# Attention layers: the output product recorded in eight planned pieces between the rounds, and the last two groups of the second layer tile by tile

## The chip, the cores and the metric

The kernel runs on one core of one Trainium2 chip. The metric is device microseconds of one execution; less is better. It is given as the median of several runs.

## The reference, cut to what matters

Three transformer layers run one after the other on 256 tokens (two tiles of 128) of width 1024, all in 32-bit floats. The change touches the ends of the first two, each of which is attention over 16 heads of width 64, an output product, and a residual sum:

```python
# layer A (top-k picked keys), dsa_mixer
out = lax.map(block, ...)              # softmax(q k + bias, masked) v, by block of 128 queries
out = from_blocks(out).reshape(b, s, A_HEADS * A_HEAD_DIM)
return out @ w_o                       # 1024 x 1024
# layer B (low-rank keys and queries), mla_mixer
out = from_blocks(out).reshape(b, s, B_HEADS * V_DIM)
return out @ w_o                       # 1024 x 1024
# first_block, for both
h = h + mixer(rms_norm(h, g), ...)
h = h + sq_relu_mlp(rms_norm(h, mlp_norm[layer]), mlp_w_up[layer], mlp_w_down[layer])
```

A third layer (gated recurrence and windowed attention) and its feed-forward follow; the change leaves them as they are.

## The kernel before, in words

The code records instructions; a scheduler then orders each engine's list, with code that is recorded earlier as the more urgent, and sets the waits. Every engine works its own list from front to back.

**Products.** Every weight block of 512 rows by 512 columns (1 MB) is loaded by SyncE into a `raw` buffer and split in two halves: `whi` = a rounded copy, two ACT instructions of 1024 columns (L252), and `wlo` = `raw` minus `whi`, two DVE instructions (L255). There are 3 `raw` and 4 `whi`/`wlo` buffers. The other operand is split the same way after its transposes (L169: the high part on ACT, the low part on DVE). A product is three matmuls for each 128 rows: hi·hi (L275), hi·lo (L276), lo·hi (L278), 512 columns each, into one of two `acc` banks.

**Attention.** `att_step` (layer A) and `attend` (layer B) cut attention into steps of three functions: f1 makes logits (`lg`), the row maximum (`mx`, `nb`, `nx` on DVE) and the exponentials (`p` or `lg` on ACT, L493); f2 transposes them (`tr`, L165) and copies the result to `pT`, in turn on ACT (L500) and DVE (L502); f3 multiplies by the values into the one `po` bank (L509). `stages` runs f1 of a step beside f2 of the step before and f3 of the one before that; one such turn is a round. A finished half of 512 features is divided by the row sums (`o` L697, `oB` L888), transposed and split into `oT` (`aoh`/`aol` in layer A, `boh`/`bol` in layer B). There are two `tr` banks and three `lg` banks.

**Order.** `weave` walks a plan, a string: a star is a round, `*4` four of them, `**` the rest; the other words are items: projections, `k3` and `q3` (layer B's products for head group 3), `33` (transposes of its keys and queries into `KTb` and `QT`, L846 and L850), `o10` (transposes of tile 1, half 0). `out_proj` follows as one call, after the whole plan: it loads the four weight blocks of `w_o`, then computes for each tile both halves of the outputs over all eight feature blocks, and adds each to the residual `h` (L318). The MLP that follows takes the first weight blocks of `mlp_w_up` in the buffers that `w_o` leaves, and norms, transposes and splits `h` (`hn` L191, `mxh`/`mxl` L169).

Of the kernel before, what the change touches and what calls it, by code (L numbers as in the profile page):

```python
# [24 lines left out]
NACC, NTR, NLG, NPO = 2, 2, 3, 1  # L25


PLAN_A = "s0 k0 q0 q1 t00 t01 s1 * t10 k1 *4 t11 **"
PLAN_B = "k0 q0 k2 20 q1 k1 30 21 *2 q2 31 * 22 k3 q3 *2 32 *4 23 *2 o00 33 *5 o10 *2 o01 o11"
PLAN_C = "ck mg ms cq q0 mw k0 mn v0 v1 ml B0 *2 q1 *3 B1 *3 o0 k1 *3 k2 * v2 * q2 B2 o1 *2 a0 *2 a1 * b1 * p0 p1 *4 b0 *3"  # L30


# [57 lines left out]
def block_kernel(ctx: ExitStack, tc: tile.TileContext, a, out: bass.AP):  # L90
    nc = tc.nc
    V, A, G, PE = nc.vector, nc.scalar, nc.gpsimd, nc.tensor
# [9 lines left out]
    def nm(s):  # L102
        uid[0] += 1
        return f"{s}_{uid[0]}"
# [20 lines left out]
    def acc(s):  # L125
        return pp.tile([P, 512], F32, tag="acc", name=nm(s), bufs=NACC)
# [34 lines left out]
    def transposes(src, n, ps=None, w=P):  # L161

        ps = trp("tr") if ps is None else ps
        for i in range(n):
            PE.transpose(ps[:w, i * P:(i + 1) * P], src[:, i * w:(i + 1) * w], ident)  # L165
        return ps
# [32 lines left out]
    @contextmanager  # L199
    def behind(ins):  # L200

        with ExitStack() as st:
            for i in ins or ():
                st.enter_context(tc.issue_after(i.ins))
            yield

    def norm_x(x, gain, fold=True):


        holds, rs = [tuple(mark[1:])], []  # L210
        for t in range(2):
            if fold:
                rs.append(rms_stats(hres[t]))
                norm_T(hres[t], None, gain, x, t)
            else:
                norm_T(hres[t], rms_stats(hres[t]), gain, x, t)
            holds.append(tuple(mark))
        return holds, rs

    def xpair(s, kt=8):  # L220

        if kt == 2:
            b = t4(s, F32R).rearrange("p (e k n) -> p e k n", e=2, k=2)
            return [b[:, 0]], [b[:, 1]]

        def part(sfx):
            return [t4(s + sfx, F32R, n * 256).rearrange("p (k n) -> p k n", k=n)
                    for n in (min(4, kt - g) for g in range(0, kt, 4))]
        return part("h"), part("l")
# [5 lines left out]
    def xs(x, k, t):  # L235
        return x[k // 4][:, k % 4, t * P:(t + 1) * P]

    def wsplit(w, k0, kk, c0, n, gain=None, by_k=False):
        raw = wp.tile([P, 2048], F32, tag="raw", name=nm("raw"), bufs=NRAW)
        hi = wp.tile([P, 2048], F32R, tag="hi", name=nm("whi"), bufs=NHL)  # L240
        lo = wp.tile([P, 2048], F32R, tag="lo", name=nm("wlo"), bufs=NHL)
        m = kk * n
        if by_k:
            for k in range(kk):
                nc.sync.dma_start(raw[:, k * n:(k + 1) * n], w[(k0 + k) * P:(k0 + k + 1) * P, c0:c0 + n])
        else:
            nc.sync.dma_start(raw[:, :m].rearrange("p (k n) -> p k n", k=kk),
                              w[k0 * P:(k0 + kk) * P, c0:c0 + n].rearrange("(k p) n -> p k n", p=P))
        if gain is None:
            for i in range(2):  # L250
                c = slice(i * m // 2, (i + 1) * m // 2)
                A.activation(hi[:, c], raw[:, c], AF.Copy)  # L252
            for i in range(2):
                c = slice(i * m // 2, (i + 1) * m // 2)
                V.tensor_tensor(lo[:, c], raw[:, c], hi[:, c].bitcast(F32), op=OP.subtract)  # L255
        else:
            for k in range(kk):
                c = slice(k * n, (k + 1) * n)
                gk = gain[:, k0 + k:k0 + k + 1]
                A.activation(hi[:, c], raw[:, c], AF.Copy, scale=gk)  # L260
                V.scalar_tensor_tensor(lo[:, c], raw[:, c], gk, hi[:, c].bitcast(F32), op0=OP.mult, op1=OP.subtract)
        v = lambda x: x[:, :m].rearrange("p (k n) -> p k n", k=kk)
        return v(hi), v(lo)

    def wparts(w, KT, c0, n, k0=0, gain=None, by_k=False):
        return [(g, min(4, KT - g), wsplit(w, k0 + g, min(4, KT - g), c0, n, gain, by_k and g == 0))
                for g in range(0, KT, 4)]

    def mm_tok(o, x, t, parts, KT):

        xh, xl = x
        for g, kk, (wh, wl) in parts:
            for k in range(kk):
                s0 = xs(xh, g + k, t)
                PE.matmul(o, s0, wh[:, k, :], start=(g + k == 0), stop=False)  # L275
                PE.matmul(o, s0, wl[:, k, :], start=False, stop=False)  # L276
            for k in range(kk):
                PE.matmul(o, xs(xl, g + k, t), wh[:, k, :], start=False, stop=(g + k == KT - 1))  # L278
# [9 lines left out]
    def dense_by_tile(jobs, holds=(None, None)):  # L288

        parts = []  # L290
        for (_, KT, w, c0, n, gain, _), hold in zip(jobs, holds):
            with behind(hold):
                parts.append(wparts(w, KT, c0, n, gain=gain))
        for t in range(2):
            for pr, (x, KT, _, _, n, _, evac) in zip(parts, jobs):
                ps = acc("acc")
                mm_tok(ps[:, :n], x, t, pr, KT)
                evac(t, ps[:, :n])

    def out_proj(x, w, scale=None, holds=(None, None)):  # L300
        dense_by_tile([(x, 8, w, 512 * ci, 512, None, lambda t, ps, ci=ci: add_res(t, ci, ps, scale))
                       for ci in range(2)], holds)
# [12 lines left out]
    def add_res(t, ci, ps, scale=None):  # L315
        h = hres[t][:, ci * 512:(ci + 1) * 512]
        if scale is None:
            V.tensor_tensor(h, ps, h, op=OP.add)  # L318
        else:
            V.scalar_tensor_tensor(h, ps, scale, h, op0=OP.mult, op1=OP.add)  # L320
# [191 lines left out]
    def stages(steps, skew=(0, 1, 2)):  # L512


        for i in range(len(steps) + skew[-1]):
            for k, d in enumerate(skew):
                if 0 <= i - d < len(steps):
                    steps[i - d][k]()
            yield
# [5 lines left out]
    def weave(plan, items, steps):  # L525

        rounds = stages(steps)
        for f in plan.split():
            if f == "**":
                for _ in rounds:  # L530
                    pass
            elif f[0] == "*":
                for _ in range(int(f[1:] or 1)):
                    next(rounds, None)
            else:
                items[f]()
        assert next(rounds, rounds) is rounds
# [36 lines left out]
    def layer_a():  # L574
        w = a["a_w_in"][0]
# [14 lines left out]
        x = xpair("ax")  # L590
        holds, rs = norm_x(x, None)
# [4 lines left out]
        for ci in range(2):  # L596
            for t in range(2):
                ps = acc("acc")
# [7 lines left out]
        for t in range(2):  # L606
# [11 lines left out]
            ps = transposes(dup.rearrange("p a b d -> p (a b d)"), 4)  # L618
            V.tensor_copy(KT[:, :, t * P:(t + 1) * P], ps.rearrange("p (a n) -> p a n", a=4))
            ps = transposes(kv[:, 128:640], 4)  # L620
# [8 lines left out]
        picked = [None, None]  # L629
# [47 lines left out]
        def q_T(t, ci):  # L677
            tp = transposes(qn[t, ci], 4)
            A.activation(qT[t][:, ci * 512:(ci + 1) * 512], tp, AF.Copy)

        oT = xpair("ao")
        steps = []
        lnx = [(sm("l", 16), sm("nx", 16)) for t in range(2)]
        for th in '00 01 10 11'.split():
            t, half = int(th[0]), int(th[1])
# [15 lines left out]
        items = {}  # L701
        for i in range(2):
            items["s%d" % i] = lambda i=i: scores(i)
            items["k%d" % i] = lambda i=i: topk(i)
            items["q%d" % i] = lambda i=i: dense(x, 8, w, [(512 * i, 512)], lambda t, _, ps: ev_q(t, i, ps), gain=gcol)
            for ci in range(2):
                items["t%d%d" % (i, ci)] = lambda i=i, ci=ci: q_T(i, ci)
        weave(PLAN_A, items, steps)
        out_proj(oT, a["a_w_o"][0], holds=picked)

    identb = cp.tile([P, P], BF, name="identb")
    V.tensor_copy(identb, ident)
# [1 line left out]
    def layer_b():  # L714
# [32 lines left out]
        holds, rs = norm_x(xb, None)  # L747
# [42 lines left out]
        def ev_dq(t, ps):  # L790
# [3 lines left out]
                      holds=(None, holds[1]))  # L794

        oB = [t4("oB") for _ in range(2)]
        scq, kvs, made = {}, {}, {}
# [95 lines left out]
        oT = xpair("bo")  # L893

        def o_T(t, i):
            tp = transposes(oB[t][:, i * 512:(i + 1) * 512], 4).rearrange("p (k n) -> p k n", k=4)
            put(oT, i, t, tp)

        items, steps = {}, []
        for gi in range(4):  # L900
            for c, f in zip("kq23", proj(gi)):
                items[c + str(gi)] = f
        for c in '00 01 10 11 20 21 30 31'.split():
            steps += attend(int(c[0]), int(c[1]))
        for t in range(2):
            for i in range(2):
                items["o%d%d" % (t, i)] = lambda t=t, i=i: o_T(t, i)
        weave(PLAN_B, items, steps)
        out_proj(oT, a["b_w_o"][0], holds=(made[2], made[3]))

    def block2():
        w = a["w_in_2"][0]
# [380 lines left out]
    layer_a()  # L1293
    mlp(0)
    layer_b()
    mlp(1)
    block2()
# [28 lines left out]
```

## Time and profile before

| | |
|---|---|
| median of 3 runs | 1156.35 us (1152.83 to 1156.69) |
| the profiled execution's own time | 1153.44 us |
| its span, first to last instruction | 1151.3 us |
| what lies around the span | 2.14 us |
| TensorE busy | 1124.7 us (98%) |
| VectorE, ScalarE busy | 678.6 us (59%), 614.1 us (53%) |
| mean granted TensorE clock | 0.998 of full speed |

The work of layer A's attention lies at 60 to 120 us of the span, that of layer B's at about 340 to 416 us. Busy time of TensorE (PE) counts matmuls that overlap in the pipeline, so the starts of instructions say more than the sum.

### The profile page before, as it was taken

How to read it: one execution, taken by the hardware profiler on the slowest of the kernel's cores; microseconds unless marked ns; L12 is line 12 of the kernel's file. 1: busy time of each engine (PE TensorE's matmuls, PEld its weight loads, DVE VectorE, ACT ScalarE, POOL GpSimd, SP SyncE). 2: the span in 40 equal slices, each digit the busy share in tenths (PEclk: the TensorE clock that was granted, in tenths of full speed). 3: DMA queues.
4: the chain of work that ended last, by engine and by line, in shares of the span. 5: the costliest groups of instructions: out<-in, count | busy, mean ns of one | idle time of the engine just before them, and what ended most of it. 6: DMA issues, size and time to landing. Idle time of an engine off the chain costs nothing.

```text
span 1151.3 us, 17271 instructions
## 1 busy us (share of the span) xinstructions
PE 1124.7 (98%) x6912; PEld 992.4 (86%) x6912; DVE 678.6 (59%) x1224; ACT 614.1 (53%) x1070; POOL 68.4 (6%) x80
## 2 busy tenths in 40 slices
PE   7989999999998999999999999999999999999997
PEld 6767898889897879989989999888888878999996
DVE  6794754445688574554366976645475566544544
ACT  7654555445487555554446664555554435433443
POOL 1210000000043000000000000010000030000000
PEclk9999999999999999999999999999999999999999
DMA  9540646554462346565538444744544535546641
GB/s 282 199 147 23 216 151 222 182 184 132 132 212 75 104 147 214 170 219 184 171 107 281 147 147 148 240 143 147 183 147 153 183 122 178 206 154 213 202 141 61
DMA packets 105383, 191.92 MB, mean 167 GB/s; under 512 B 6616, under 2 KB 22960, under 8 KB 105304
## 3 DMA queue, kind: packets, MB, share of 16 engines
q1 hardware_dynamic: 104056, 187.16, 48.6%
q0 software_dynamic: 1040, 3.54, 1.0%
q8 instruction: 54, 0.88, 0.3%
q14 instruction: 25, 0.20, 0.1%
q10 hardware_dynamic: 208, 0.13, 0.0%
HBM read 189.68 MB, written 1.13 MB: 166 GB/s over the span
## 4 chain that ended last, share of the span: by engine, by line
PE 92%; DVE 4%; ACT 1%; issue 1%; DMA 0%; POOL 0%; SPq 0%; POOLq 0%; DVEq 0%; ACTq 0%
PE acc L275 10%; PE acc L276 10%; PE acc L278 9%; PE dn L361 7%; PE dn L362 7%; PE dn L364 7%; PE up L310 5%; PE up L313 5%; PE up L311 5%; PE tr L165 3%; PE po L509 2%; PE qk L310 2%; PE qk L311 2%; PE lg L485 2%; PE qk L313 2%; PE fp L310 1%
## 5 line engine op out<-in xcount | busy, mean ns | idle before, releaser
L255 DVE TENSOR_TENSOR wlo<-raw,whi 128x1024 fp32r<-128x1024 f32 (+3 forms) x340 | 385.5, 1177 | 211.3 <-ACT whi L252 211.1
L252 ACT ACTIVATE whi<-raw 128x1024 fp32r<-128x1024 f32 (+3 forms) x340 | 322.9, 1007 | 212.3 <-PE dn L364 86.7
L310 PE MATMUL up<-mxh,whi 128*128 128x256 f32 x448 | 110.9, 281 | 0.0
L311 PE MATMUL up<-mxl,whi 128*128 128x256 f32 x448 | 110.7, 280 | 0.0
L361 PE MATMUL dn<-whi,uh 128*128 128x512 f32 x256 | 100.7, 395 | 0.0
L362 PE MATMUL dn<-wlo,uh 128*128 128x512 f32 x256 | 100.6, 394 | 0.0
L158 POOL TENSOR_TENSOR rr<-rv,mhalf 128x1 f32<-128x1 f32 (+2 forms) x42 | 39.8, 950 | 821.5 <-DVE rv L156 806.2
L310 PEld LDWEIGHTS up<-mxh,whi 128*128 128x128 f32 x448 | 84.3, 188 | 0.7
L311 PEld LDWEIGHTS up<-mxl,whi 128*128 128x128 f32 x448 | 84.2, 188 | 0.7
L275 PE MATMUL acc<-whi,cxh 128*128 128x512 f32 (+1 forms) x192 | 74.5, 389 | 0.0
L276 PE MATMUL acc<-wlo,cxh 128*128 128x512 f32 (+1 forms) x192 | 72.3, 378 | 0.0
L313 PE MATMUL up<-mxh,wlo 128*128 128x256 f32 x448 | 71.0, 280 | 0.0
L364 PE MATMUL dn<-whi,ul 128*128 128x512 f32 x256 | 69.5, 394 | 0.0
L313 PEld LDWEIGHTS up<-mxh,wlo 128*128 128x128 f32 x448 | 60.3, 188 | 0.0
L361 PEld LDWEIGHTS dn<-whi,uh 128*128 128x128 f32 x256 | 48.1, 188 | 13.2 <-ACT whi L252 2.6
L364 PEld LDWEIGHTS dn<-whi,ul 128*128 128x128 f32 x256 | 48.1, 188 | 11.2
L362 PEld LDWEIGHTS dn<-wlo,uh 128*128 128x128 f32 x256 | 48.1, 188 | 10.6
L278 PE MATMUL acc<-whi,cxl 128*128 128x512 f32 (+1 forms) x192 | 50.6, 382 | 0.0
L169 DVE TENSOR_TENSOR ul<-sq,uh 128x512 fp32r<-128x512 f32 x28 | 19.4, 692 | 51.8 <-ACT uh L169 51.5
L310 PE MATMUL qk<-cxh,whi 128*128 128x256 f32 x192 | 49.1, 287 | 0.0
L311 PE MATMUL qk<-cxl,whi 128*128 128x256 f32 x192 | 48.2, 282 | 0.0
L493 ACT ACTIVATE lg<-lg,nx 128x128 f32<-128x128 f32 (+1 forms) x80 | 35.4, 446 | 16.3 <-DVE nx L553 16.3
(414 smaller groups left out, 2410.2 us busy)
## 6 DMA issues: line engine op xcount, KB each, us to landing
raw<-in_w_in SPq DMA_DIRECT2D x38, 1024.0 KB, 5.2
raw<-in_mlp_w_up SPq DMA_DIRECT2D x32, 1024.0 KB, 5.3
raw<-in_mlp_w_down SPq DMA_DIRECT2D x32, 1024.0 KB, 5.1
raw<-in_w_gate SPq DMA_DIRECT2D x10, 1024.0 KB, 5.5
raw<-in_w_up SPq DMA_DIRECT2D x10, 1024.0 KB, 5.1
raw<-in_w_down SPq DMA_DIRECT2D x10, 1024.0 KB, 5.0
raw<-in_w_in SPq DMA_DIRECT2D x6, 688.0 KB
raw<-in_a_w_in SPq DMA_DIRECT2D x4, 1024.0 KB
```

Of the source, the lines that this page charges most:

```text
L158: G.tensor_tensor(r[:, :n], v[:, :n], mhalf[:, :n], op=OP.pow)
L252: A.activation(hi[:, c], raw[:, c], AF.Copy)
L255: V.tensor_tensor(lo[:, c], raw[:, c], hi[:, c].bitcast(F32), op=OP.subtract)
L275: PE.matmul(o, s0, wh[:, k, :], start=(g + k == 0), stop=False)
L276: PE.matmul(o, s0, wl[:, k, :], start=False, stop=False)
L278: PE.matmul(o, xs(xl, g + k, t), wh[:, k, :], start=False, stop=(g + k == KT - 1))
L310: PE.matmul(o, s0, xh[(g + k) // 4][:, (g + k) % 4, :], start=(g + k == 0), stop=False)
L311: PE.matmul(o, s0, xl[(g + k) // 4][:, (g + k) % 4, :], start=False, stop=False)
L313: PE.matmul(o, wl[:, k, col:col + P], xh[(g + k) // 4][:, (g + k) % 4, :], start=False, stop=(g + k == KT - 1))
L361: PE.matmul(ps, s0, wh[:, k, :], start=(c == 0 and k == 0), stop=False)
L362: PE.matmul(ps, s0, wl[:, k, :], start=False, stop=False)
L364: PE.matmul(ps, xs(u[1], k, t), wh[:, k, :], start=False, stop=(c == nc_ - 1 and k == kt - 1))
```

## The change

The call of `out_proj` in the two layers goes. In its place a new function puts ten items into the plan: `w0`, `w1` load and split the weight blocks for the two halves of the outputs; `m` with three digits is the part of the product for a tile, a half of the outputs and a half of the features (four feature blocks, 12 matmuls). The second feature half adds the result to `h`. The plans set the items between the rounds. In layer B the steps of the last two head groups run tile by tile: 20, 30, 21, 31 in place of 20, 21, 30, 31.

```diff
-PLAN_A = "s0 k0 q0 q1 t00 t01 s1 * t10 k1 *4 t11 **"
-PLAN_B = "k0 q0 k2 20 q1 k1 30 21 *2 q2 31 * 22 k3 q3 *2 32 *4 23 *2 o00 33 *5 o10 *2 o01 o11"
+PLAN_A = "s0 k0 q0 q1 t00 t01 s1 * t10 k1 *4 t11 w0 w1 *6 m000 * m001 * m010 * m011 * m100 * m110 ** m101 m111"
+PLAN_B = "k0 q0 k2 20 q1 k1 30 21 *2 q2 31 * 22 k3 q3 *2 32 *3 23 * o00 33 w0 w1 *2 o10 *3 o01 m000 * m001 * m010 * m011 * m100 m110 o11 m101 m111"
+    def out_parts(items, x, w, holds):
+        parts, banks = {}, {}
+        def load(ci):
+            with behind(holds(ci)):
+                parts[ci] = wparts(w, 8, 512 * ci, 512)
+        def run(t, ci, gi):
+            if gi == 0:
+                banks[t, ci] = acc("acc")
+            g, kk, (wh, wl) = parts[ci][gi]
+            ps = banks[t, ci]
+            for k in range(kk):
+                s0 = xs(x[0], g + k, t)
+                PE.matmul(ps, s0, wh[:, k, :], start=(g + k == 0), stop=False)
+                PE.matmul(ps, s0, wl[:, k, :], start=False, stop=False)
+            for k in range(kk):
+                PE.matmul(ps, xs(x[1], g + k, t), wh[:, k, :], start=False, stop=(g + k == 7))
+            if gi == 1:
+                add_res(t, ci, ps)
...
+        out_parts(items, oT, a["a_w_o"][0], lambda ci: picked[ci])
         weave(PLAN_A, items, steps)
-        out_proj(oT, a["a_w_o"][0], holds=picked)
...
-        for c in '00 01 10 11 20 21 30 31'.split():
+        for c in '00 01 10 11 20 30 21 31'.split():
             steps += attend(int(c[0]), int(c[1]))
...
+        out_parts(items, oT, a["b_w_o"][0], lambda ci: made[2 + ci])
         weave(PLAN_B, items, steps)
-        out_proj(oT, a["b_w_o"][0], holds=(made[2], made[3]))
```

No instruction is added or taken away; the lists of SyncE and GpSimd stay as they were. In layer A the list of VectorE stays too, and the others differ in few places. Lines of the changed kernel below `out_parts` are 28 higher (L500 is L528, L868 is L896).

ScalarE at the end of layer A, before. `pT_1004` holds the last transposed probabilities of tile 1, the last input that `po` needs; `whi_1204` and `whi_1212` are the first two weight blocks of the MLP; `aoh_394` is the last split of layer A's result.

```order
L500 ACTIVATE pT_974<-tr_969 128x512
L500 ACTIVATE pT_1004<-tr_999 128x512
L252 ACTIVATE whi_1204<-raw_1203 128x1024 x2
L252 ACTIVATE whi_1212<-raw_1211 128x1024 x2
L169 ACTIVATE aoh_394<-tr_1018 128x4x128
```

The same place now (`pT_1114` is the former `pT_1004`):

```order
L528 ACTIVATE pT_1058<-tr_1053 128x512
L252 ACTIVATE whi_1204<-raw_1203 128x1024 x2
L252 ACTIVATE whi_1212<-raw_1211 128x1024 x2
L528 ACTIVATE pT_1114<-tr_1109 128x512
L169 ACTIVATE aoh_394<-tr_1128 128x4x128
```

The last `pT` copy stands behind the four splits of the MLP's weights. TensorE at that place, now (`acc_1065` and `acc_1096` are the two output halves of tile 1, `whi_779` and `whi_795` the weight blocks whose buffers `whi_1204` and `whi_1212` take):

```order
L165 MATMUL tr_1085<-ident,lg_1045 128x128 x4
L319 MATMUL acc_1065<-whi_779,aol_395 128x512 x4
L537 MATMUL po_1060<-kvi_178,pT_1058 128x64
...
L319 MATMUL acc_1096<-whi_795,aol_395 128x512 x4
L165 MATMUL tr_1109<-ident,lg_1045 128x128 x4
L537 MATMUL po_1060<-kvi_178,pT_1090 128x64
...
L537 MATMUL po_1060<-kvi_178,pT_1114 128x64
```

Before, `po` and the four transposes of `tr_999` stood ahead of both L278 groups; now the first group stands ahead of `po`, and `tr_1109` behind both.

VectorE in layer B, now, behind the `QT` copies of head group 3. Before, the reduces `mx` of tile 0 of that group stood between the second and third and between the third and fourth of the `wlo` pieces.

```order
L878 COPY QT_2834<-tr_3792 96x512
L878 COPY QT_2834<-tr_3798 96x512
L255 TENSOR_TENSOR wlo_3822<-raw_3820,whi_3821 128x1024 x2
L255 TENSOR_TENSOR wlo_3830<-raw_3828,whi_3829 128x1024 x2
L530 COPY pT_3846<-tr_3843 128x256
L896 TENSOR_REDUCE mx_3112<-lg_3855 128x2
L896 TENSOR_REDUCE mx_3112<-lg_3878 128x2
L896 TENSOR_REDUCE mx_3115<-lg_3895 128x2
L169 TENSOR_TENSOR bol_3090<-tr_3871,boh_3088 128x4x128
L897 TENSOR_TENSOR nb_3113<-mx_3112,scq_3598 128x2 x2
```

All four pieces now run in one go. ScalarE at the end of layer B, before and now (`boh_3089` is the second feature half, its second row tile 1; `whi_4151` and `whi_4159` are the MLP's first weight blocks):

```order
L169 ACTIVATE boh_3089<-tr_3958 128x4x128
L169 ACTIVATE boh_3089<-tr_3965 128x4x128
L175 ACTIVATE sq_4367,ss_845_4366<-h_70 128x512
L175 ACTIVATE sq_4369,ss_845_4366<-h_70 128x512
L252 ACTIVATE whi_4151<-raw_4150 128x1024 x2
L252 ACTIVATE whi_4159<-raw_4158 128x1024 x2
```

```order
L169 ACTIVATE boh_3089<-tr_3930 128x4x128
L528 ACTIVATE pT_4022<-tr_4017 128x512
L175 ACTIVATE sq_4367,ss_845_4366<-h_70 128x512
L175 ACTIVATE sq_4369,ss_845_4366<-h_70 128x512
L252 ACTIVATE whi_4151<-raw_4150 128x1024 x2
L169 ACTIVATE mxh_4110<-tr_4116 128x4x128
L252 ACTIVATE whi_4159<-raw_4158 128x1024 x2
L169 ACTIVATE boh_3089<-tr_4075 128x4x128
L169 ACTIVATE mxh_4111<-tr_4124 128x4x128
```

Tile 1's last split now stands behind the MLP's weight splits.

## Rows read from the trace of the kernel before

**Rows 1.** The page: span, busy time of each engine, and the chain by engine.

```profile
span 1151.3 us, 17271 instructions
PE 1124.7 (98%) x6912; PEld 992.4 (86%) x6912; DVE 678.6 (59%) x1224; ACT 614.1 (53%) x1070; POOL 68.4 (6%) x80
PE 92%; DVE 4%; ACT 1%; issue 1%; DMA 0%; POOL 0%; SPq 0%; POOLq 0%; DVEq 0%; ACTq 0%
```

**Rows 2.** Stretches of 1 us: PE, PEld, DVE, ACT, POOL busy; PEclk; DMA.

```profile
101.00:102.00 1.00, 0.19 (x2) 0.06 (x1) 0.97 (x3) 0.72 (x2) 0.00 (x0) 1.00 0.00 0
369.00:370.00 1.00, 1.00 (x5) 0.96 (x5) 1.00 (x4) 0.39 (x3) 0.00 (x0) 0.50 0.00 0
```

**Rows 3.** Timeline of PE, end of layer A: start, us, operation [idle before].

```profile
109.66 2.10 PE L278 MATMUL acc<-whi,aol 128*128 128x512 f32 x8
111.60 1.89 PE L509 MATMUL po<-kvi,pT 128*128 128x64 f32 x16
114.28 0.66 PE L165 MATMUL tr<-ident,o 128*128 128x128 f32 x4 [0.79 <-DVE o L697]
```

**Rows 4.** Timeline of ACT, end of layer A.

```profile
110.00 0.60 ACT L500 ACTIVATE pT<-tr 128x512 f32<-128x512 f32 x1 [5.75 <-PE tr L165]
110.88 3.90 ACT L252 ACTIVATE whi<-raw 128x1024 fp32r<-128x1024 f32 x4 [0.28 <-PE acc L278]
```

**Rows 5.** The chain that ended last, layer B: start, us held, engine, tile, line.

```profile
369.83 1.71 PE lg L867 x4
...
374.45 0.86 PE lg L867 x4
375.31 1.73 PE po L509 x16
...
378.22 0.44 PE tr L165 x4
...
402.54 1.84 PE acc L278 x8
```

**Rows 6.** Timeline of PE in layer B.

```profile
365.77 0.44 PE L165 MATMUL tr<-ident,p 128*128 128x128 f32 x2 [0.82 <-DVE QT L850]
...
368.03 0.94 PE L509 MATMUL po<-kvb,pT 128*128 128x64 f32 x4 [0.71 <-DVE pT L502]
...
373.68 0.77 PE L165 MATMUL tr<-ident,p 128*128 128x128 f32 x2 [1.19 <-ACT p L493]
...
378.86 0.48 PE L275 MATMUL acc<-whi,boh 128*128 128x512 f32 x1
...
391.21 0.77 PE L165 MATMUL tr<-ident,p 128*128 128x128 f32 x2 [0.49 <-ACT p L493]
...
398.55 0.50 PE L275 MATMUL acc<-whi,boh 128*128 128x512 f32 x1 [0.17 <-ACT boh L169]
...
416.83 0.51 PE L275 MATMUL acc<-whi,mxh 128*128 128x512 f32 x1 [0.25 <-ACT mxh L169]
```

**Rows 7.** Timeline of DVE in layer B.

```profile
371.96 0.68 DVE L502 COPY pT<-tr 128x512 f32<-128x512 f32 x1
...
372.65 0.20 DVE L869 TENSOR_TENSOR nb<-mx,scq 128x2 f32<-128x2 f32 x2
...
382.82 1.28 DVE L850 COPY QT<-tr 96x512 f32<-96x512 f32 x2 [3.31 <-PE tr L165]
384.02 2.35 DVE L255 TENSOR_TENSOR wlo<-raw,whi 128x1024 fp32r<-128x1024 f32 x2
...
386.89 0.41 DVE L868 TENSOR_REDUCE mx<-lg 128x2 f32<-128x256 f32 x1
```

**Rows 8.** Timeline of ACT in layer B.

```profile
378.69 0.68 ACT L846 ACTIVATE KTb<-tr,bgkq 96x512 f32<-96x512 f32 x1 [0.35 <-PE tr L165]
...
390.61 0.46 ACT L493 ACTIVATE p<-lg,nb,scq 128x128 f32<-128x128 f32 x1 [4.21 <-DVE nb L869]
...
397.90 1.11 ACT L169 ACTIVATE boh<-tr 128x512 fp32r<-128x512 f32 x2 [1.64 <-PE tr L165]
```

More of the change, by code (lines that the diff above doesn't have):

```diff
@@ L298, in dense_by_tile @@
                 evac(t, ps[:, :n])
+    def out_parts(items, x, w, holds):
[16 more added lines that the diff above has]
+                add_res(t, ci, ps)
+        for ci in range(2):
+            items["w%d" % ci] = lambda ci=ci: load(ci)
+            for t in range(2):
+                for gi in range(2):
+                    items["m%d%d%d" % (t, ci, gi)] = lambda t=t, ci=ci, gi=gi: run(t, ci, gi)
     def out_proj(x, w, scale=None, holds=(None, None)):
```

## The prediction

> **What bounds the kernel now.** The page comes first [rows 1]: TensorE (PE) is busy 98% of the span, and the chain that ended last runs through PE for 92% of it. So the kernel ends when PE has worked off its list, and a change that moves instructions without adding any can only give or take time in which PE waits or runs at the lower clock. VectorE (DVE) and ScalarE (ACT) matter only through such waits. The ends of the two attention layers are read next, in the timelines of PE, DVE and ACT side by side, then the chain for what an instruction costs PE in a row of its like.
>
> In that row [rows 5] a matmul of 512 columns in a product holds PE 0.23 us (1.84 for 8), a transpose 0.11 (0.44 for 4), a pass of `po` 0.11 (1.73 for 16), four passes of `lg` of 256 columns 0.86. One thing more is to be seen: at 369.83 us four such passes took 1.71 us. The granted clock there is 0.50 [rows 2], the lower of the two levels, 1.2 GHz. It followed two waits of PE close together, 0.82 and 0.71 us, with little work around them [rows 6]. Near 101 us PE stood for most of a microsecond too, and the clock stayed at 1.00 [rows 2].
>
> DVE and ACT take their instructions strictly as listed. The trace shows what that costs. In layer B the second `QT` copy ended at 384.1 [rows 7], and the logits that need it take PE under a microsecond; but DVE's list had two `wlo` pieces next, from 384.02, so `mx` started at 386.89 [rows 7], and with two more pieces between the reduces ACT stood 4.21 us for `nb` [rows 8]. PE lost only 0.49 us then, since it had a quarter of the output product to do [rows 6].
>
> **What could be won.** In layer B, PE waits 1.19, 0.49, 0.17 and 0.25 us between 373 and 417 us [rows 6], and the slow `lg` passes lose 0.85 us: 2.95 us together if the new order filled them all. The scheduler had already put the product's pieces among the rounds (L275 starts at 378.86, 20 us before the second feature half at 398.55), so naming eight pieces is new in the plan more than on the engine.
>
> That bound stands against a rule of the Trainium skill. "Perfetto Trace Analysis", in "Optimization Strategy", says that work of stages with different limits may gain by being interleaved. By that rule the sum would be the gain of at most 2.95 us; by the steps below it is a loss.
>
> **Layer A.** What moves: the first four L278 matmuls of tile 1 go ahead of `po`, one `pT` copy on ACT goes behind four weight splits. Times are those of the trace. Before, eight L278 matmuls start at 109.66 and the first split at 110.88, 1.22 us later, when the first four have ended and given their buffer back [rows 3, 4]. Ahead of them stood four transposes and eight `po` passes, 1.3 us. Without those the first four start at about 108.4, and the splits at 109.6. One split takes 0.97 us (3.90 for 4). The second pair needs the buffer of the other four matmuls; with eight `po` passes between (0.87) these end near 111.4, so the pair follows without a gap and ends at 113.5. Then comes the copy, 0.60 us [rows 4]: 114.1. PE has then long done the four transposes and the first eight of the sixteen `po` passes, at about 112.5, and needs the copy for the other eight, which before started at 111.60 + 0.87 = 112.5 [rows 3]. **So +1.6 us**, a new wait on PE. Behind it stand the division `o`, its transposes (which wait 0.79 us as before), the last split, and all that follows; none has slack, since the MLP's first product starts from them. The bounds of this wait are 0, if the copy were done first, and 2.5 us, two splits and a copy in full. I take the walk's value because its buffers and durations all stand in rows.
>
> **Layer B.** Up to the reduces before 372 us DVE's list is the same, so this walk starts there; times again as in the trace, without the 1.6 us.
> - First piece. `pT` ends at 372.64 and `nb` at 372.85 [rows 7]. The next `oB` (a pass over 256 columns, 0.41) now follows at once, where a reduce of 512 columns stood, so `po` starts at 373.3. Sixteen passes and two transposes, 1.95, end at 375.25. The transposes of the next keys wait for a `tr` bank that ACT frees: four exponentials from 372.9 (0.46 each [rows 8], a little less in a row), then `KTb`, 0.68 [rows 8]: 375.3. With four transposes the first output piece starts at 375.8. Before: 378.86 [rows 6]. 3.0 us ahead.
> - Logits. PE then does 12 matmuls of the piece, 8 transposes, a matmul and two transposes, 4.1 us: 379.95. The second `QT` copy follows its transposes and ends near 380.4, a wait of 0.45. Then 1.75 us of logits, 11 matmuls and 6 transposes: 385.4. DVE has four `wlo` pieces in one go behind `QT`, 4.6 us, then `pT`: also 385.4. PE does eight `po` passes to 386.3 and needs the exponentials of group 3. They wait for three reduces (0.34, 0.34, 0.60: in a row, a DVE pass takes some 0.07 less than alone), a `bol` (0.60) and `nb` on DVE, 387.4, and one exponential, 387.9. **PE waits 1.6 us**, where it waited 0.49 before at 391.21. Still 3.3 us ahead.
> - To the second feature half: some 7.4 us of transposes, logits and `po`, with about 0.45 us of short waits: 395.75. Before: 398.55. 2.8 us ahead; what had been done later (a reduce, logits of tile 1) has caught up.
> - From there to the MLP's first matmul, before: 72 matmuls (16.8), eight transposes and 0.25 of waiting in 18.3 us, 416.83. Now 16 `po` passes and eight more transposes stand here as well, 2.6. And tile 1's last split, `boh`, stands behind the second weight block's splits on ACT, which need a buffer that PE gives back only at the end of tile 1's first half. From that moment ACT takes two splits and `boh`, 1.95 + 0.60 with the signals some 2.7; PE has six transposes, 0.66. **A wait of 2.1 us.** Before, `boh` was done at 397.90 to 399 [rows 8], long ahead. Then DVE has the low part, four `wlo` pieces, another low part and the sum into `h`, each of the three 0.60, 6.4 us; only that frees the bank for the MLP. PE has 24 matmuls, 5.6: a wait of 0.8 in place of 0.25. 18.3 + 2.6 + 2.1 + 0.6 = 23.6: 419.3. **So +2.5 us** at the MLP.
>
> The bounds for layer B: -2.95 us, all old waits gone and no new one; +5.1, the new waits of 0.45, 1.6, 2.1 and 0.8 and small ones with nothing won. The value is nearest the upper end since two of the three are weight splits ahead of an operand, as in layer A.
>
> **Edits at nothing.** The loads of `w_o` and of the MLP's weights keep their place on SyncE's queue, and GpSimd's list is the same; ACT waits for buffers that PE frees, not for loads. If a load came late, its 1 MB would stand ahead of the splits. The MLP's inner steps are the same and shift as one; if a buffer there were given back late, the slow start would show in its first 10 us.
>
> **The sum.** 1.6 + 2.5 = 4.1 us on the profiled execution: 1153.44 + 4.1 = 1157.5. That execution lies 2.9 us under the median; on the median, 1156.35 + 4.1 = **1160.5**, 0.35% slower. About 0.5%, 5.8 us, is what a measurement of this kernel can tell from no change, so the forecast falls under "same" though I expect a loss.
>
> **Rivals.**
> - *The clock (slower).* The new waits are longer than the two before 368 us, and two lie close behind sparse work: 1.6 in layer A with 0.79 right behind, 1.6 in layer B amid short matmuls. If one makes the clock fall, PE runs at half speed as from 368 to 372: 3.5 us, in dense products 1.75 lost. One fall makes 5.85, at the bound; two 7.6: 1162 to 1164. For it: the row at 369. Against it: 101 us, and that the fall at 368 now strikes work that waits anyway. It decides from the first fall on that strikes dense work. Chance 0.29. The Trainium skill, "TensorE: Matmul & The Clock Gate", in "A second HAM failure mode: psum-queue depth-cycling", says that an engine that stops briefly and often between groups of matmuls can swing between its clocks. The trace agrees with it at one place, the fall after two short waits, and not at 101 us; by that rule this rival would come out.
> - *The pieces fill the holes (faster in sign).* If ACT and DVE reach the new places early, the waits of layers A and B don't appear and up to 2.95 us come back: 1153.4. For it: ACT is busy only 53%. Against it: the splits can't start before PE frees their buffers. Chance 0.10.
> - *It doesn't do what it says.* Layer A's VectorE list is unchanged and PE's nearly so; with ACT's four splits hidden and layer B's gain and loss equal: 1156 to 1157. Chance 0.08.
>
> The forecast has the remaining 0.53.
>
> **How the numbers follow.** Slower by over 0.5%: most of the clock's 0.29 and 0.05 of the forecast's spread (the 4.1 is good to about 1.5, and a median of three moves by about 2): 0.32. Faster by over 0.5%: 0.02 of the second rival. Same: 0.66. The range: below, the filled holes and a median from the low end of the runs, 1155.5; above, two falls of the clock, 1164.
>
> **What would show it.** In layer A, PE waits 1.5 to 2 us at `po` for ACT's `pT`, behind four splits. In layer B the first L275 starts about 3 us earlier against the layer's start, PE waits about 1.6 us for an exponential, about 2 us at L275 (there L316) for `boh`, and the MLP's first product starts 4 us later than at 416.83. Wrong: no wait of PE over 1 us for ACT at these three places; or granted clock of 0.5 in more stretches, which speaks for the first rival; or a shift of the MLP that doesn't reach the end.

## The result and the profile after

The changed kernel takes **1163.8 us** (median of 7 runs, 1162.33 to 1166.44); the kernel before took 1156.35 us beside it (7 runs, 1152.83 to 1159.63). The ratio is 1.0078, 95% interval 1.0062 to 1.0095: slower, by 7.45 us. The forecast was 1160.5 us, "same"; the time lies within its range, at the upper end, where the rival on the clock had put it (1162 to 1164).

The page of the changed kernel, span, PE and the chain by engine, to be set against [rows 1]:

```profile
span 1162.0 us, 17266 instructions
...
PE 1130.7 (97%) x6912; PEld 997.5 (86%) x6912; DVE 678.1 (58%) x1224; ACT 614.7 (53%) x1070; POOL 68.0 (6%) x80
...
PE 90%; DVE 5%; ACT 2%; issue 1%; DMA 1%; POOL 0%; SPq 0%; POOLq 0%; DVEq 0%
```

The instructions are the same. PE's busy time grew by 6.0 us, so the same matmuls ran slower, and the part of the chain on DVE and ACT grew, that is, waits of PE. The end of layer A, first PE's timeline, with a line of the kernel before behind it, then ACT's:

```profile
115.28 1.10 PE L537 MATMUL po<-kvi,pT 128*128 128x64 f32 x8 [1.38 <-ACT pT L528]
117.17 0.66 PE L165 MATMUL tr<-ident,o 128*128 128x128 f32 x4 [0.79 <-DVE o L725]
...
119.11 0.63 PE L317 MATMUL acc<-wlo,aoh 128*128 128x512 f32 x1
```

```profile
115.95 0.39 PE L276 MATMUL acc<-wlo,aoh 128*128 128x512 f32 x1
```

```profile
110.85 3.90 ACT L252 ACTIVATE whi<-raw 128x1024 fp32r<-128x1024 f32 x4 [5.34 <-PE acc L319]
114.66 0.57 ACT L528 ACTIVATE pT<-tr 128x512 f32<-128x512 f32 x1
```

Where [rows 3, 4] had the copy first and the four splits behind it, the splits are first, and PE stands 1.38 us for the copy. Behind it the second 512-column matmul of the product takes 0.63 us, where the same one took 0.39 before. The stretches of 1 us say why (PE, PEld, DVE, ACT, POOL busy; granted clock; DMA share and GB/s):

```profile
109.00:110.00 1.00, 1.00 (x8) 0.81 (x8) 0.08 (x1) 0.00 (x0) 0.00 (x0) 1.00 0.00 0
...
119.00:120.00 1.00, 1.00 (x4) 0.71 (x4) 1.00 (x2) 0.25 (x1) 0.00 (x0) 0.50 0.00 0
...
374.00:375.00 1.00, 0.40 (x2) 0.00 (x0) 1.00 (x2) 0.51 (x1) 0.00 (x0) 0.50 0.80 242
...
383.00:384.00 1.00, 1.00 (x3) 0.73 (x3) 0.00 (x0) 1.00 (x2) 0.00 (x0) 0.50 0.00 0
384.00:385.00 1.00, 1.00 (x8) 0.83 (x7) 0.00 (x0) 1.00 (x2) 0.00 (x0) 1.00 0.00 0
```

The clock is at 0.50 (1.2 GHz) for 3.4 us from 117.8 on, and in layer B for 10.2 us, to 384.0; before it was there for 3.4 us in layer B and not at all in layer A [rows 2]. In layer B, PE's timeline against [rows 6]:

```profile
371.43 0.66 PE L537 MATMUL po<-kvb,pT 128*128 128x64 f32 x4 [0.72 <-DVE pT L530]
...
375.14 0.69 PE L165 MATMUL tr<-ident,oB 128*128 128x128 f32 x2 [0.75 <-ACT pT L528]
...
381.32 0.78 PE L316 MATMUL acc<-whi,boh 128*128 128x512 f32 x1
...
394.62 0.77 PE L165 MATMUL tr<-ident,p 128*128 128x128 f32 x2 [1.40 <-ACT p L521]
...
419.51 0.50 PE L316 MATMUL acc<-whi,boh 128*128 128x512 f32 x1 [1.85 <-ACT boh L169]
...
425.98 0.50 PE L275 MATMUL acc<-whi,mxh 128*128 128x512 f32 x1 [0.63 <-DVE h L346]
```

The waits are the ones forecast: 1.40 us for an exponential (1.6), 1.85 for `boh` (2.1), 0.63 for the sum (0.8). ACT shows the split standing behind two pairs of weight splits:

```profile
413.74 2.01 ACT L252 ACTIVATE whi<-raw 128x1024 fp32r<-128x1024 f32 x2 [2.46 <-PE acc L319]
...
416.97 2.00 ACT L252 ACTIVATE whi<-raw 128x1024 fp32r<-128x1024 f32 x2 [0.75 <-PE acc L319]
418.88 0.58 ACT L169 ACTIVATE boh<-tr 128x512 fp32r<-128x512 f32 x1
```

Three marks cut every span into four parts: the first `po` of layer A, the first product `acc<-whi,mxh` of its MLP, and the last such product of layer B's MLP (some 12 us into that MLP; its other products lie in the rest). One row of each kernel has the last two. Before, then after:

```profile
L275 PE MATMUL acc<-whi,mxh x32: 388/396/505, 122.2 to 428.7; 128*128 128x512 f32 x32
```

```profile
L275 PE MATMUL acc<-whi,mxh x32: 389/393/505, 125.7 to 438.5; 128*128 128x512 f32 x32
```

With the first `po` at 66.3 and 67.6 us, the 10.7 us between the spans are 1.3 before layer A's first `po` (executions of the kernel before differ as much there), **2.2 in A, 6.3 in B and 0.9 in the rest**. All experiments are read by these parts. Of the changed kernel's seven executions three took 1166.3 to 1166.4 us; none of them was profiled, and what parts them from the other four stays open.

### The profile page after: what moved, and what is told of

It reads as the page before. It is cut to its first block, busy times and chain, and to the rows that moved or that the text cites. A ratio compares the mean times of both kernels' runs of the same rounds, so it can differ in the third digit from the quotient of the medians.

```text
span 1162.0 us, 17266 instructions
## 1 busy us (share of the span) xinstructions
PE 1130.7 (97%) x6912; PEld 997.5 (86%) x6912; DVE 678.1 (58%) x1224; ACT 614.7 (53%) x1070; POOL 68.0 (6%) x80
## 4 chain that ended last, share of the span: by engine, by line
PE 90%; DVE 5%; ACT 2%; issue 1%; DMA 1%; POOL 0%; SPq 0%; POOLq 0%; DVEq 0%
PE acc L275 8%; PE acc L276 8%; PE acc L278 8%; PE dn L389 7%; PE dn L390 7%; PE dn L392 7%; PE up L338 5%; PE up L339 5%; PE up L341 5%; PE tr L165 3%; PE po L537 2%; PE qk L339 2%; PE qk L338 2%; PE qk L341 2%; PE lg L513 2%; DVE wlo L255 2%
## 5 line engine op out<-in xcount | busy, mean ns | idle before, releaser
L278 PE MATMUL acc<-whi,cxl 128*128 128x512 f32 (+1 forms) x192 | 50.5, 382 | 0.0
L175 ACT ACTIVATE sq<-h 128x512 f32<-128x512 f32 x28 | 17.5, 627 | 52.1 <-DVE h L346 25.5
```

## The experiments

**Theory:** two weight splits put ahead of an operand on ACT, and the clock, which falls behind the waits. **Rivals:** the waits alone; the group order; the clock as a property of the run and not of the change.

**1. One layer at a time.** Old plan, group order and `out_proj` in layer B, or in layer A.

```diff
# e1_a_only: PLAN_B, the order '00 01 10 11 20 21 30 31' and out_proj(oT, a["b_w_o"][0], ...) as before
# e2_b_only: PLAN_A and out_proj(oT, a["a_w_o"][0], holds=picked) as before
```

> Layer A as in the changed kernel, layer B with the old plan, group order and output product. Waits and clock: PE waits 1.4 us at po for ACT's pT behind four weight splits, the granted clock falls to 0.50 for one stretch near 118 us, the MLP of layer A starts 2.3 us later; the median lies 2 to 2.5 us over the kernel before, layer B is the old one shifted. Waits alone, the low clock being no cost: +1.6 us. Nothing in layer A reaches the end: 0.

> Layer B as in the changed kernel, layer A as before. Waits and clock: the same waits as in the changed kernel (1.4 us for an exponential, 1.9 us for boh, 0.6 us for the sum into h) and some 10 us at a granted clock of 0.50 from about 371 us; +5.5 to 6 us over the kernel before. Waits alone: +2.5 us and the clock low for no longer than the 3.5 us of before. If the clock in layer B falls so long only because layer A's change has shifted it, this run has the old 3.5 us.

e1: 1160.07 against 1156.93 us, 1.0031 (1.0016 to 1.0046). e2: 1161.49, 1.0056 (1.0038 to 1.0075). The two add up (3.1 + 4.6 us). e2 has the three waits of the changed kernel (1.40, 1.85 and 0.63 us) and the 10.2 us at 0.50, with 3.4 us more at 392, though layer A is the old one; so the fall in layer B is not layer A's doing. It lies under the 5.5 to 6 that were expected. e1 is over its 2 to 2.5, and its layer B is not "the old one shifted": the same instructions take 310.7 us between the marks instead of 306.5, since its clock is low for 10.2 us there and not for 3.4. So the profile of before had shown only one of the ways in which its own layer B runs, as the next part confirms.

**2. The kernel before, in other executions.**

> The kernel before, unchanged, looked at once more. Its executions lie in two groups, 1153 to 1154 us at a mean granted clock of 0.998 and 1158 to 1159 us at 0.994, and the profile shown of it is of the first. If the low stretch in layer B is what parts them, an execution of the second group shows 10 us at 0.50 from about 368 us in place of 3.4; one of the first shows the 3.4 again. If they are parted elsewhere, the stretch at 368 us is 3.4 us long at either time.

> The kernel before once more, unchanged. At 1153 to 1154 us: one stretch of 3.4 us at 0.50 in layer B and none earlier. At 1156 to 1157: a second stretch in layer A, as in e5_before_again, or 6.8 us in layer B. At 1158 to 1159: about 10 us in layer B from 368 to 372 us on, as e1_a_only has behind the same instructions. If an execution of 1158 to 1159 shows 3.4 us there, the groups have another cause.

> As e16_before_third: the same kernel, another execution, the same reading of its time against the length of its stretches at 0.50.

Of 103 executions of the kernel before in the four comparisons, 42 took 1152.9 to 1154.6 us, 20 took 1155.9 to 1157.3 and 41 took 1157.7 to 1159.8. Four profiles of it, and e1:

| execution | time | part A | low clock in A | part B | low clock in B |
|---|---|---|---|---|---|
| the first profile | 1153.44 | 55.9 | 0 | 306.5 | 3.4 us |
| e16 | 1153.61 | 55.9 | 0 | 306.2 | 0 |
| e5 | 1156.07 | 57.2 | 3.4 us, from 77.3 | 306.5 | 3.4 us |
| e17 | 1156.92 | 55.9 | 0 | 309.5 | 6.8 us |
| e1, the same layer B | 1160.12 | | | 310.7 | 10.2 us |

e5's expectation named layer B alone; that execution lost its time in layer A. e16, expected with one stretch, has none; e17 is as expected. The same list with the same data thus has no, one or a longer stretch at 0.50, and in these profiles the time of the part follows the length. A stretch of 3.4 us at 368 costs 0.3 (it strikes PE where it waits anyway), 6.8 cost 3.3, 10.2 cost 4.5 against e16. No execution at 1158 to 1159 was profiled; that it is one of 10.2 us is inferred from e1. Nine of e1's 12 executions have the mean clock of its profile, 0.992, while 41 of 103 of the kernel before lie in the slowest group; a median that has the long stretch more often would explain why e1 is over layer A's 2.2. e17's windows of 2 us, with the 2.26 us wait for an exponential before the fall, and then those of e16, which has nearly the same wait (2.08 us) and no fall:

```profile
372.00:374.00 2.00, 0.00 (x0) 0.00 (x0) 2.00 (x7) 1.03 (x4) 0.00 (x0) 1.00 1.05 408
...
378.00:380.00 2.00, 2.00 (x12) 2.00 (x12) 0.60 (x2) 0.70 (x2) 0.00 (x0) 0.50 0.04 8
380.00:382.00 2.00, 2.00 (x11) 1.97 (x11) 0.69 (x1) 0.97 (x2) 0.00 (x0) 0.50 0.00 0
```

```profile
372.00:374.00 2.00, 0.12 (x1) 0.13 (x1) 2.00 (x7) 1.22 (x4) 0.00 (x0) 1.00 1.06 401
...
378.00:380.00 2.00, 2.00 (x16) 1.86 (x16) 1.12 (x2) 1.22 (x3) 0.00 (x0) 1.00 0.00 0
```

e1 has the very waits of e16 at this place (0.63, 0.71, 0.24 and 2.08 us) and is low for 10.2 us behind them. So the waits alone do not decide whether the clock falls in an execution; what does stays open.

**3. Matmuls that nobody reads, in PE's waits.** They multiply the identity into a free PSUM bank, behind a given transpose.

```diff
+def fill(n, ins, bank):
+    ps = bank("fl")
+    with behind([ins]):
+        for _ in range(n):
+            PE.matmul(ps, identb, identb[:, None, :].to_broadcast([P, 4, P]), start=True, stop=True)
# e6, e7: 3 behind the QT transposes of group 2, 3 and 4 behind the second p transposes of (1, 0) and (1, 1); e13: 9 for the 4
# e10: in layer A, 5 behind the last p transposes, 3 behind the last po
```

> The kernel before, with ten matmuls of 512 columns into a free accumulation bank, whose result nobody reads, in the places of layer B where PE stood 0.82, 0.71 and 1.19 us (three, three and four, 0.23 us each at the full clock). If the clock falls there because PE has too little to do: no stretch at 0.50 in layer B in any execution, all of them at about 0.998 or more, median 1152.5 to 1154 us, 3 to 4 us under the kernel before, though PE has 2.3 us more to do. If the fall does not hang on PE's own work: the two groups stay, and the median is that of before or up to 2.3 us more.

> e6_fill_before with nine matmuls in place of four at the third place, where PE still stood 1.21 us for an exponential and the clock fell 1.9 us later in the profiled execution. If the remaining falls hang on that wait, no execution has a stretch at 0.50 in layer B: one group, 1153 to 1154.3 us, and the spread of the kernel before, 1153 to 1159 us, is shown to be this clock. If they come from the short matmuls behind it, the second group at 1156 us stays and the median is 1154 to 1156 us.

e6: 1154.22 us, 0.9984 (0.9969 to 1.0), half met: four of its 11 executions take 1155.9 to 1156.5 us, and the one of them that was profiled falls for 6.8 us behind the 1.21 us wait that was left. e13: **1154.08 us, 0.998 (0.9966 to 0.9994)**, all 12 executions from 1152.9 to 1154.43. It beats the medians of both kernels, with some 3.5 us of useless matmuls (15 at 0.23) in it, and lies where the first group of the kernel before lies. Its timeline and windows at the place of e17's wait and fall:

```profile
370.91 2.10 PE L722 MATMUL fl<-identb 128*128 128x512 bf16 x9
373.32 0.77 PE L169 MATMUL tr<-ident,p 128*128 128x128 f32 x2 [0.31 <-ACT p L497]
```

```profile
372.00:374.00 2.00, 1.58 (x8) 0.67 (x7) 1.75 (x7) 1.28 (x6) 0.00 (x0) 1.00 1.04 374
374.00:376.00 2.00, 2.00 (x17) 1.89 (x16) 1.15 (x4) 1.71 (x9) 0.00 (x0) 1.00 0.98 345
...
378.00:380.00 2.00, 2.00 (x14) 1.73 (x13) 1.12 (x2) 0.69 (x1) 0.00 (x0) 1.00 0.00 0
380.00:382.00 2.00, 2.00 (x13) 1.61 (x12) 0.00 (x0) 0.90 (x2) 0.00 (x0) 1.00 0.00 0
```

> The changed kernel with the same ten matmuls at the same places of layer B. If the clock is the rest of its loss: no 10 us at 0.50 in layer B, the one at 118 us stays; 3 to 5 us off, 1159 to 1160.5 us, and what is left over the kernel with the fillers is the waits and layer A, 5 to 6 us. If the clock is no cost: 1164 to 1166 us.

> e1_a_only with eight matmuls of 512 columns, read by nobody, where PE waits in layer A: five in the 1.4 us at po, three in the 0.8 us ahead of the transposes of o. If those waits make the clock fall near 118 us, it stays at 1.00 and 0.7 us come off: 1159.3, the MLP of layer A at +1.7 us in place of +2.3 against the same start. Layer B keeps its own falls. If the clock falls there for another reason: no change, 1160.

e7: 1160.56 us, 1.003 (1.0017 to 1.0043), 3.2 off the changed kernel, as expected; its part B is 309.6 for 312.8. The 10.2 us are gone, but its profile falls for 3.4 us at 417, behind the 1.85 us wait for `boh` that was left. In the new order the mean clock says less than in the old: e2's six executions are not ordered by it (1160.8 us at 0.993, 1161.68 at 0.996). e10: 1158.94, 1.0027 (1.0012 to 1.0041), 1.1 off e1 (0.5, each set against the kernel before measured beside it). Part A goes from 58.1 to 57.5, so of layer A's 2.2 us, 0.6 is the clock and 1.6 the wait. The windows of e1 and then of e10:

```profile
116.00:118.00 2.00, 1.84 (x9) 1.60 (x10) 0.30 (x2) 0.60 (x1) 0.00 (x0) 0.59 0.11 34
118.00:120.00 2.00, 2.00 (x6) 1.57 (x7) 2.00 (x3) 0.60 (x1) 0.00 (x0) 0.56 0.00 0
```

```profile
116.00:118.00 2.00, 1.61 (x11) 0.95 (x9) 0.62 (x2) 0.74 (x2) 0.00 (x0) 1.00 0.10 34
118.00:120.00 2.00, 2.00 (x9) 1.66 (x10) 2.00 (x3) 0.35 (x1) 0.00 (x0) 1.00 0.00 0
```

**4. The weight splits put behind the operand on ACT.**

```diff
 def mlp(i):
-    holds = [tuple(mark[1:])]
+    holds = [tuple(mark)]          # e3: in the changed kernel; e9: in e2_b_only
```

> The changed kernel, with the splits of the MLP's first weights put behind the last operand split of each attention layer on ACT. The waits of 1.4 us at po (layer A) and 1.9 us for boh (layer B) go. Waits and clock: layer A comes back to the kernel before, its fall of the clock near 118 us with it; layer B keeps the 10 us at 0.50, since they come before the boh wait; together 4 us off the changed kernel, still about 3 over the kernel before. If the two weight splits ahead of an operand are not what costs, under 1 us comes off; if they cost all, the kernel before is reached.

> Layer B as in the changed kernel, layer A as before, and the splits of the MLP's first weights put behind the last operand split on ACT. Against e2_b_only it takes away only the wait of 1.8 us for boh, and gives part of that back at the sum into h: 1.0 to 1.6 us off, 1160 to 1160.5 us. That leaves some 3 us over e8_order_clean, of which 1.1 us lie behind 680 us. If the boh wait is all that parts e2_b_only and e8_order_clean, it is e8_order_clean's 1156.9.

e3: 1161.12 us, 1.0047 (1.0029 to 1.0066), 2.7 off and not the 4 expected: the waits of 1.4 and 1.9 are gone and part A is 56.4, but in that profile layer B is low for 13.7 us (10.2 and 3.4 later), and PE waits 1.1 for the sum into `h`. e9: 1160.1, 1.0038 (1.0025 to 1.0051), 1.4 off e2, within what was expected (0.8, each set against the kernel before measured beside it): the wait for `boh` is 0.25, the one for the sum into `h` 1.08. In its profile layer B is low for 6.8 us where e2's is for 13.7, so not all of this need be the split's.

**5. The group order alone.** With the old plan kept as it was:

> The kernel before with the group order of the changed kernel in layer B (20 30 21 31) and nothing else. If the two tile-0 groups in a row leave PE with little work between short waits at 371 to 376 us and so make the clock fall: 7 to 10 us at 0.50 there, a wait of over 1 us for an exponential near 392 us, +3 to 4.5 us at the MLP, but no wait of 1.9 us for boh. If the eight named pieces make the fall and the waits: as the kernel before, within 1 us.

In it group 3's first logits come before its keys and queries are written, and use what lies in those buffers; so its 1160.97 us, 1.0045 (1.0028 to 1.0063), say nothing on the kernel. The clean one moves the items too:

```diff
-PLAN_B = "... *2 32 *4 23 *2 o00 33 *5 o10 *2 o01 o11"
+PLAN_B = "... *2 32 *3 23 * o00 33 *2 o10 *3 o01 *4 o11"
```

> The kernel before with the group order 20 30 21 31 and the four transposes of the outputs where the changed kernel has them, but the output product in one call behind the rounds, as before; layer A as before. On PE, DVE and ACT the scheduler then lists layer B within a few rows of the changed kernel's order. So if the group order is the change and the naming of eight pieces is nothing, it is e2_b_only over again, 1160.5 to 1162 us, with a shorter wait for boh, since that split then stands ahead of the second pair of weight splits. If the pieces make the loss, it is the kernel before, 1156 to 1157 us.

1156.85 us, 0.9996 (0.9983 to 1.001). That is the time of the second half of the expectation, so the pieces make the loss; but it is not the kernel before over again, since its clock falls as in e2 (10.2 us from 368, 3.4 at 392). From 370 to 404 us its PE runs within 0.15 us of e2. Then come the rows in which the lists differ; ACT of e8, against the rows of the changed kernel above, and the starts of the MLP's product in e8 and then, with the wait for `boh`, in e2:

```profile
410.82 2.01 ACT L252 ACTIVATE whi<-raw 128x1024 fp32r<-128x1024 f32 x2 [1.85 <-PE acc L278]
412.74 0.58 ACT L169 ACTIVATE mxh<-tr 128x512 fp32r<-128x512 f32 x1
413.21 0.59 ACT L169 ACTIVATE boh<-tr 128x512 fp32r<-128x512 f32 x1
414.26 2.01 ACT L252 ACTIVATE whi<-raw 128x1024 fp32r<-128x1024 f32 x2 [0.46 <-PE acc L278]
```

```profile
420.42 0.50 PE L275 MATMUL acc<-whi,mxh 128*128 128x512 f32 x1 [0.19 <-DVE h L318]
```

```profile
416.56 0.50 PE L316 MATMUL acc<-whi,boh 128*128 128x512 f32 x1 [1.85 <-ACT boh L169]
...
423.02 0.50 PE L275 MATMUL acc<-whi,mxh 128*128 128x512 f32 x1 [0.63 <-DVE h L346]
```

One place in ACT's list (PE transposes tile 1's outputs a little earlier, so `boh` can stand between the two pairs of weight splits): `boh` is done as PE comes to it, and the MLP's first product starts at 420.42 us where e2 has 423.02. So the pieces cost 2.6 us there, 2.3 of them in these two waits, and 1.3 in the rest of the span (722.1 against 723.4). e9, with both pairs behind `boh`, has a part B of 311.1 where e8 has 310.8 and e2 313.6, but with half of their low clock; its rest is e2's (723.6).

> e8_order_clean, whose executions have about 10 us and then 3.4 us at a granted clock of 0.50 in layer B, with nine of the matmuls that nobody reads, three at each of the first three waits (0.81, 0.72 and 0.75 us). If the clock is what keeps the group order from paying: the first stretch gone or one step of 3.4 us long, 1152.5 to 1154.5 us, under both kernels. If the stretch only moves behind the fillers, as in e6_fill_before's profile: 1155.5 to 1156.5 us.

> e11_order_fill with seven more such matmuls behind the outputs of tile 0 of the third group, ahead of its 1.89 us wait for an exponential near 388 us, after which the clock fell for 3.4 us. If that wait makes the fall: no stretch at 0.50 left in layer B, 1.7 us off, 1153 to 1154 us. If the seven stand in the way of the transposes and logits behind them: 1155 to 1156 us.

e11: 1154.91 us, 0.999 (0.9977 to 1.0004), between its two forecasts, all 12 executions within 1154.47 to 1155.6: the first stretch is gone, 3.4 us near 390 are left, behind a wait of 1.89 us. e15: 1155.55, 0.9991 (0.9978 to 1.0005): the seven ran behind that wait and not in it, so they stand in the way, the fall stays near 389, and whether the wait makes it was not tried. No profile shows the new order with the clock up throughout. By an estimate from e11, whose 3.4 us at half speed can cost up to 1.7, it would be at most 0.9 us ahead of the old order with its waits filled (e13); a gain is not shown.

**6. The changed kernel with both repairs,** e3 with the nine matmuls of e11.

> The changed kernel with both repairs: the splits of the MLP's first weights behind the last operand split (e3_splits_behind) and nine matmuls that nobody reads at the first three waits of layer B. If the two ACT inversions and the clock are the loss, the first gives 2.7 us off 1163.8 (e3_splits_behind) and the second 3.3 us (e7_fill_after): 1157 to 1158.5 us, the rest over the kernel before being the longer qk products and the wait at the sum into h. If the two gains are the same one, it stays at 1160 to 1161 us.

1158.59 us, 1.0018 (1.0005 to 1.0032): the repairs give 5.2 us together, 2.7 and 3.2 alone. 2.2 over the kernel before are left. Its profile still has the 1.89 us wait for an exponential with 3.4 us at 0.50 behind it (from 391), 1.07 us of wait for the sum into `h`, and a rest of 723.0.

**7. The rest of the span.** From the last mark to the end, all kernels with the old layer B take 722.6 us (but for e12) and the clean order 722.1, with the pieces it is 723.0 to 724.0. In the changed kernel the 0.9 lie in the products `qk` of the fourth block, in which PE has no wait; first and last start of one form before, after and in e12:

```profile
L310 PE MATMUL qk<-cxh,whi x192: 277/280/472, 677.6 to 819.1; 128*128 128x256 f32 x192
```

```profile
L338 PE MATMUL qk<-cxh,whi x192: 275/283/470, 687.5 to 829.9; 128*128 128x256 f32 x192
```

```profile
L310 PE MATMUL qk<-cxh,whi x192: 276/280/469, 680.4 to 822.3; 128*128 128x256 f32 x192
```

> The kernel before with one scratch tile held over the start of the fourth block, so that its input's high and low parts lie in other SBUF buffers: the first half in the two that it has in the changed kernel, e2_b_only and e3_splits_behind, which are 1.1 us longer than the rest between 684 and 830 us without a wait of PE. If the place of the tiles is the cause, the products qk of this run are longer by about as much (half of it, if only the second half's place counts: 0 to 0.5). If not, they are as long as in the kernel before, 141.9 us from first to last.

141.5 us before, 142.4 after, 141.9 in e12 (1156.8 us in one execution; rest 723.2). The 141.9 that the expectation gives for the kernel before is not the time between these starts, which is 141.5. The change releases tiles in another order, and so the block's input gets other buffers; a scratch tile that does the same to the kernel before gives about half of the effect. The kernels sort by these buffers: all that keep those of the kernel before take 141.4 to 141.7 us, the clean order among them, and the changed kernel, e2, e3 and e9, which share another set, take 142.4. e7 and e14 have, among the input's four buffers, only that of the second low part other than those four kernels, and take 141.9. So the time goes with the place, and half of it with that one buffer; why stays open.

## Why the prediction was right or wrong

- **Layer A, +1.6:** right. The copy stands behind four splits, PE waits 1.38, and without the fall of the clock part A is 1.6 us longer (e10).
- **Layer B, +2.5:** nearly right. At the same 10.2 us of low clock, B is 312.8 in the changed kernel and 310.7 with the old list (e1): +2.1, though the 10.2 us strike other rows there. The three late waits came 0.17 to 0.25 us shorter than forecast; with the clock up before it, the one for the exponential is 1.89 (e7).
- **The early lead of 3.0, 3.3 and 2.8 us:** wrong for this execution. The first piece starts at 381.32; less the 3.40 by which layer B was entered later (`tr` with the `QT` wait, 369.17 for the 365.77 of [rows 6]) that is 0.9 ahead of 378.86. The clock took the lead: in e7, where it is up until 417, the first piece starts 10.0 us behind that transpose where the kernel before needs 13.1, so 3.1 ahead, and the next two leads are 3.3 and 2.0. No gain followed from the lead: e8 is no faster than the kernel before, and e11 and e15, with 3.4 us of low clock left, are not faster than e13.
- **"Naming eight pieces is new in the plan more than on the engine":** right for the first part of layer B and wrong in effect: up to the MLP e8 and e2 differ by a few rows, and in all by 4.6 us.
- **What could be won, at most 2.95:** not tested, since the matmuls of e13 fill the old waits without doing any of the kernel's work; nothing of it was won by the change. By the rule of the Trainium skill, "Perfetto Trace Analysis", "Optimization Strategy", the interleaving might have gained; no run here shows a gain from it.
- **The step that failed** is the sum "1156.35 + 4.1": it has the waits alone, and the term of the clock stands in it at nothing, left to a rival of 0.29. It carried the clock of one profiled execution (3.4 us, harmless) over to both sides. The changed kernel is low for 3.4 us in A, +0.6, and for 10.2 in B in the profiled execution, and no execution of it has a mean clock over 0.995, while 42 of 103 of the kernel before were free of the cost. Added to that are 0.9 us in the rest, which no step had: "can only give or take time in which PE waits or runs at the lower clock" does not hold for the products `qk`. From profile to profile the 10.7 us are 1.3 before layer A, 1.6 + 2.1 of waits (4.1 forecast), 0.6 + 4.2 of the clock and 0.9 in the rest. The medians lie 7.45 apart, since the median of the kernel before has a part of the clock's cost in it too.
- **The clock rival** came out in its total, not in its parts: two falls at 1.75 each were priced; they cost 0.6 and 4.2 (10.2 us in place of 3.4; by e7 the clock in B is worth at least 3.2). That the time fell into its 1162 to 1164 is in part luck, since the 0.9 us of the rest were needed for it. Its argument against itself, that the fall at 368 us strikes work that waits anyway, holds for the first 3.4 us (e16) and not for a longer stretch. The rule of the Trainium skill that is named with it ("TensorE: Matmul & The Clock Gate", "A second HAM failure mode: psum-queue depth-cycling") agrees with e10 in layer A and e13 in layer B: with the stops filled, the clock stays up at 1.00. e16 has the stops and no fall, so they need not bring one.

## What to carry to other kernels

Before the terms of a sum are set against a median, look at several executions of the kernel before: where its times lie in groups and the mean granted clock differs with them, one profile is one of the groups. Where an operand's split, a copy or an exponential shares an in-order list with weight splits, a piece of product that moves ahead frees buffers early, and the weight splits pass the operand; name the operand's split as what the first weight split must stand behind, and look at what then comes late (here the sum, 1.08 us). Where PE waits a microsecond amid short matmuls, matmuls that nobody reads in the wait can cost less than the clock that they keep; here that paid in full only where all the long waits were filled (e13), and in e6, e7, e11 and e14 the clock fell behind the next one that was left.

## What was not expected of the hardware

The same list on the same data has 0, 3.4, 6.8 or (with layer A changed) 10.2 us at 1.2 GHz in layer B, for 306.2, 306.5, 309.5 and 310.7 us. Two profiles with the same waits at that place (e16 and e1) have 0 and 10.2 us of it. And products without any wait took 0.9 us in 141.5 longer with their input in other SBUF buffers, half of it going with a single one of them.
